# Second MLP up projection: eleven block-product groups on unscaled operands, the norm's row factor multiplied onto outputs

## The chip, the cores and the metric

The kernel runs on one core of a Trainium2 chip. The metric is the device time of one execution in microseconds (us); lower is better. Engine names are those of the profile: PE is TensorE (matmuls), PEld its weight loads, DVE is VectorE, ACT is ScalarE, POOL is GpSimd, SP is SyncE. POOL and SP only issue DMA transfers here. L1068 means line 1068 of the kernel before.

## The reference

One sequence of 512 tokens with 1024 channels goes through two layers: attention and a gated MLP, then a gated short convolution and a gated MLP. Every part has an RMSNorm in front and adds its result to the running state h. The change concerns the second MLP and what stands around it:

```python
def rms_norm(x, g):
    y = xf * lax.rsqrt(jnp.mean(xf * xf, axis=-1, keepdims=True) + EPS)
    return (y * g.astype(jnp.float32)).astype(x.dtype)

def conv_ffn(h, norm_g, w_up, conv_w, w_down):     # D_MODEL 1024, D_FF 2816
    xn = rms_norm(h, norm_g)
    u = causal_dwconv(xn @ w_up, conv_w)            # three taps along the tokens
    g, val = u[..., :D_FF], u[..., D_FF:]
    return (jax.nn.silu(g) * val) @ w_down
```

The norm is a gain for each channel times one factor for each token, 1/sqrt(mean square + EPS). That token factor (the "row factor") commutes with the product by w_up, so it can be multiplied onto xn before the product or onto the outputs behind it. The gain cannot.

## The kernel before, in words

**Numbers.** All data is float32. PE works on operands that are split into two halves, hi (rounded) and lo (the rest), and each product is three matmuls: hi by hi, hi by lo, lo by hi. A weight tile of 128x1024 is split by one ACT copy (whi, L1016) and one DVE subtraction (wlo, L1018). Three buffers of each half turn over.

**The stages.** Layer 0 is attention with its out projection, then MLP 0. Layer 1 is the short convolution (`conv_seven`) with its out projection, then MLP 1. Activations lie transposed, channels on the 128 partitions and the 512 tokens along the free axis.

**Up projection.** The 2816 + 2816 output channels are cut into HF = 11 groups. A group is two 128-channel tiles of the gate and two of the value. Two kinds of groups exist:

- A *plain* group (PLAIN = 2 in each MLP, ahead of the others) is four products of 1024 channels by 512 tokens, 24 matmuls of 512 columns each, with operand halves hs_a, hs_b of h times gain (L360, L361). The row factor is not needed yet; it is multiplied onto the output (`normed`, L1286). While PE works on them, the norm is finished: sums over channels by PE (L398), the reciprocal root by small DVE operations (`scale` L374, L410 to L422), and the spreading of the factor over all partitions (L384, L385).
- A *seven* group (`Sevens`, `seven` L1068) takes one 2x2 block scheme with seven half-size products, called p1, p7, p3, p6, p2, q5, q4. Each is 24 matmuls of 256 columns. Their operands are sums and differences of quarters of the normed activations (channels halved, tokens halved into LEFT and RIGHT), made once by `prepare` from h, gain and row factor (L1270, L1277), in hi and lo. Their weights are sums of blocks of w_up: X, Y, Z, three, W, four.

**The slots of a seven group** (`Sevens.slot`): slot 0 is p1 into bank A, 1 is p7 into T, 2 is p3 of the *previous* group into R, 3 is p6 into R, 4 is p2 into A, 5 is q5 into R, 6 is q4 into T. Around them stand the loads by SP (X, Y, three, W, Z), the splits of the next weights, the copies out of the banks by ACT (`to_wide` L1112 for the LEFT half of the gate yg and value yv; `kept` L1120), the joins by DVE for the RIGHT half (`join` L1115), the three-tap convolutions (`causal_conv`, first tap ACT L431, others DVE L434) and the products of gate and value (L1055, L1056).

**Weight sums.** Some are read from tables in DRAM that POOL's DMAs build ahead (`table_steps`, L102, L105; FAR = 8 steps behind attention, 16 at slot 20 of the convolution). X becomes X plus a block by a POOL DMA that adds while it writes (`add_block`, L1095). "four" is "three" plus W: in MLP 0 it is loaded from a third table, in MLP 1 it is one DVE addition in place (L1179). "three" is read by p6 before that and as "four" by q4 after it.

**The down projection** follows (L1614); its operands are made from the gated outputs, with adding POOL DMAs (L1060).

**What sets the order.** Each engine runs its own instructions in order and waits on semaphores. The order is fixed when the kernel is built, by a scheduler with a cost model; instructions marked with `keep_in_program_order` stay in the order in which the code wrote them. Tiles of a pool with a tag reuse the buffers of that tag, and wait for their last readers.

Of the kernel before, what the change touches and what calls it, by code (L numbers as in the profile page):

```python
# [25 lines left out]
P = 128  # L26
# [23 lines left out]
PLAIN = 2  # L50
FAR = 8, 16
CHUNKS = (2, 3), (5, 3), (8, 3)
# [4 lines left out]
def trunk(  # L57
# [7 lines left out]
    act, dve, pe, pool = nc.scalar, nc.vector, nc.tensor, nc.gpsimd  # L65
# [21 lines left out]
    def table_steps(layer):  # L87

        w = ffn_w_up[layer]
        for n in "76" if layer else "764":  # L90
            for g, m in CHUNKS:
                tables[layer, n, g] = far.tile([512, m * 256 + 16], F32, tag=f"t{layer}{n}{g}", name=f"t{layer}{n}{g}")
        def block(kh, half, g, m):
            return w[kh * 512:(kh + 1) * 512, half * DFF + g * 256:half * DFF + (g + m) * 256]
        for g, m in CHUNKS:
# [12 lines left out]
    def table_of(layer, n, group):  # L108
        g, m = next(c for c in CHUNKS if c[0] <= group < c[0] + c[1])
        return tables[layer, n, g][:, (group - g) * 256:(group - g + 1) * 256].rearrange("(k p) c -> p k c", p=P)  # L110
# [150 lines left out]
    brought, pin = {}, tc.keep_in_program_order  # L261
# [82 lines left out]
    class Norm:  # L344
# [27 lines left out]
        def scale(self, sums):  # L372
# [4 lines left out]
            if self.name != "n0":  # L377
                after(NROWS, self.spread)
# [17 lines left out]
        def finish(self, at=NSUMS):  # L396
            def sums(b, t):
                pe.matmul(t[:, b:b + 1], self.acc[:, b * P:(b + 1) * P], ones, start=True, stop=True)  # L398
                if b == NB - 1:
                    self.scale(t[:, 0:NB])  # L400
# [79 lines left out]
    def want_conv_out():  # L480
        for o in range(ND):
            want(conv_w_out[0], 0, 8, o * P, P)
        want_ffn(1, 2 * PLAIN)

    want_ffn(0, 2 * PLAIN)
# [501 lines left out]
    sum_far(FAR[0])  # L987
# [41 lines left out]
    class Blocks:  # L1029
# [3 lines left out]
        def __init__(self, mp, layer):  # L1033
            self.layer = layer
            self.parts = {0: mp.tile([P, HEAD, S], F32, tag="head", name=f"head{layer}")}

        def at(self, j, n):
            start = 0 if j < HEAD else HEAD if j < HF else HF
            if start not in self.parts:
                shape, tag = ([P, HF - HEAD, S], "hs_b") if start == HEAD else ([P, HF, S], "hs_a")  # L1040
                self.parts[start] = hsp.tile(shape, F32, tag=tag, name=f"{tag}_blocks{self.layer}")
# [20 lines left out]
    def seven(acc, w, x, fresh, last=True):  # L1062
# [8 lines left out]
        spend(2.8)  # L1071

    class Sevens:

        def __init__(self, name, mp, groups, block_of):
            self.name, self.mp, self.groups, self.block_of = name, mp, groups, block_of
            self.forms = {n: [mp.tile([P, 4, HT], F32R, tag=f"{n}_{i}", name=f"{n}_{i}{name}") for i in ("hi", "lo")] for n in FORMS}
            self.st, self.wides, self.table, self.fours = {}, {}, None, False
# [31 lines left out]

        def to_wide(self, g, n, side, acc):
            act.activation(self.wides[g][n][:, :, side], acc.rearrange("p (i t) -> p i t", t=HT), AF.Copy)  # L1112

        def join(self, g, n, acc, other):
            dve.tensor_tensor(  # L1115
                self.wides[g][n][:, :, RIGHT], acc.rearrange("p (i t) -> p i t", t=HT), other.rearrange("p (i t) -> p i t", t=HT), op=ALU.subtract)
# [22 lines left out]
        def slot(self, g, s):  # L1139
# [21 lines left out]
            elif s == 1:  # L1161
                first = not was
                if on and first and not self.ahead:
# [7 lines left out]
            elif s == 2:  # L1171
                if on:
                    self.kept(g, "P7s", c["T"])
                    self.weights_of(g, "p2", "W")
                    if self.fours:
                        self.load_one(g, "four", self.table("4", g))
                    else:
                        c["four"] = c["three" if self.table else "Y"]
                        dve.tensor_tensor(c["four"], c["four"], c["W"], op=ALU.add)  # L1179
# [42 lines left out]
    def up_seven(layer, norm, mp):  # L1222

        blocks = Blocks(mp, layer)
        w_up, base = ffn_w_up[layer], PLAIN
# [8 lines left out]
        up.fours = layer == 0  # L1234
        up.rate = lambda g, s: 1.4 if g == base else 0.3 if layer else 0.5

        def wides_of(g):
# [3 lines left out]
            return {n: mp.tile([P, 2, S], F32, tag=n, name=f"{n}{layer}{g}", bufs=1) for n in ("yg", "yv", "ug", "uv")}  # L1241
        up.wides_of = wides_of
        wides, forms, chores = up.wides, up.forms, up.chores
# [18 lines left out]
        up.tail = tail  # L1262
# [54 lines left out]
    def conv_seven(norm, mp):  # L1317
# [9 lines left out]
        def quarter(n, i, dt, name):  # L1327
            return mp.tile([P, 4, S], dt, tag=f"y_{n}{i}", name=name)
        early_t, early_b = (quarter(n, 0, F32, f"early_{n}") for n in ("hi", "lo"))
# [17 lines left out]
        def open_ys():  # L1347
            ys.append([quarter(n, len(ys), F32R, f"y_{n}{len(ys)}") for n in ("hi", "lo")])
# [47 lines left out]
        def prepare():  # L1396
            x0, x1 = (quarter(n, 1, F32, f"x_{n}") for n in ("hi", "lo"))
# [47 lines left out]
        for s in range(28):  # L1445
            up.slot(1 + s // 7, s % 7)
            if s == 20:
                sum_far(FAR[1])
# [6 lines left out]
        return ys  # L1455

    def mlp(layer, norm, mp):
        blocks, slots = up_seven(layer, norm, mp)
# [62 lines left out]
        n_up = 7 * (HF - PLAIN)  # L1521
        for i, fn in enumerate(slots[:n_up]):
            fn()
            left = n_up - i
# [177 lines left out]
```

## Time and profile before

| what | value |
|---|---|
| time, 3 runs | median 1123.12 us (1122.23 to 1123.92) |
| span of the profiled execution | 1119.7 us |
| median of the runs less that span | 3.4 us |
| granted TensorE clock | 90% of full speed or more in all 40 slices |
| end of the conv out projection in the trace | 779.1 us |
| MLP 1, two plain groups | 779.1 to 825.3 us |
| MLP 1, nine seven groups | 825.3 to 1001.8 us |
| down projection of MLP 1 and the end | 1001.8 to 1119.7 us |

The profiled execution has no time of its own listed beside its span; the 3.4 us between span and median are what lies around it. Start times in rows are microseconds from the start of the span. A row's duration is how long one instruction was in the engine, and because engines pipeline, neighbours may start before it is over: the cadence, start to start, is what counts for a sum. In brackets behind a row stands how long the engine was idle before it, and for whom.

### The profile page before, as it was taken

Reading aid. Unit: us, or ns where it says so; the run is one execution under the profiler, and the core shown is the slowest. Engines: PE = TensorE matmul, PEld = TensorE weight load, DVE = VectorE, ACT = ScalarE, POOL = GpSimd, SP = SyncE. Lnnn points to the kernel's source line nnn. Section 1 sums busy time; section 2 is a strip of 40 time slices with the busy share of each in tenths; the row PEclk is TensorE's granted clock in tenths of the full one; section 3 lists DMA queues with packets and bytes.
Section 4 is the critical chain, followed back from the end, with each engine's and each line's share of the span. In section 5 each row is a group of like instructions: output and inputs, shape, how many; then the busy total and the mean of one; then the engine's idle time right before and its main releaser. Section 6 shows DMA issues by size and latency. Waiting matters only on the chain.

```text
span 1119.7 us, 19368 instructions
## 1 busy us (share of the span) xinstructions
PE 1112.4 (99%) x7659; PEld 1008.0 (90%) x7659; DVE 947.8 (85%) x1463; ACT 680.0 (61%) x1013; POOL 158.4 (14%) x191
## 2 busy tenths in 40 slices
PE   9999999999999999999999999999999999999998
PEld 7888787878899999999999899988899999998876
DVE  6798988987899887888989889865899888898886
ACT  7456676655567667676547355543456766667553
POOL 4111111111111110014400001111101110014300
PEclk9999999999999999999999999999999999999999
DMA  6668878778888687699953456699877666699961
GB/s 195 171 178 193 187 185 198 167 193 207 235 207 200 184 217 192 190 304 194 225 164 91 124 142 140 147 239 227 215 185 186 168 183 152 188 266 194 233 154 57
DMA packets 175690, 209.34 MB, mean 187 GB/s; under 512 B 7564, under 2 KB 140220, under 8 KB 175600
## 3 DMA queue, kind: packets, MB, share of 16 engines
q0 software_dynamic: 41024, 86.95, 39.3%
q1 hardware_dynamic: 134416, 121.09, 34.9%
q8 instruction: 60, 0.98, 0.4%
q14 instruction: 30, 0.25, 0.1%
q10 hardware_dynamic: 160, 0.07, 0.0%
HBM read 203.10 MB, written 49.28 MB: 225 GB/s over the span
## 4 chain that ended last, share of the span: by engine, by line
PE 96%; DVE 2%; ACT 1%; issue 0%; DMA 0%; SPq 0%; DVEq 0%; ACTq 0%
PE psb L1068 28%; PE psa L1068 11%; PE psb L1614 11%; PE psa L1614 8%; PE psb L324 6%; PE psb L326 6%; PE psb L325 6%; PE psa L326 2%; PE psa L324 2%; PE psa L325 2%; PE psb L699 2%; PE psa L796 2%; PE psc L771 1%; PE psc L326 1%; PE psc L325 1%; PE psc L324 1%
## 5 line engine op out<-in xcount | busy, mean ns | idle before, releaser
L303 ACT ACTIVATE whi<-raw 128x1024 fp32r<-128x1024 f32 (+2 forms) x89 | 91.7, 1031 | 97.0 <-PE psb L325 36.6
L304 DVE TENSOR_TENSOR wlo<-raw,whi 128x1024 fp32r<-128x1024 f32 (+2 forms) x89 | 105.5, 1186 | 24.1 <-ACT whi L303 23.4
L1068 PE MATMUL psb<-p_lo,whi_p 128*128 128x256 f32 x432 | 121.6, 282 | 0.0
L1068 PE MATMUL psb<-p_hi,wlo_p 128*128 128x256 f32 x432 | 121.6, 281 | 0.0
L1068 PE MATMUL psb<-p_hi,whi_p 128*128 128x256 f32 x432 | 121.3, 281 | 0.0
L324 PE MATMUL psb<-hs_a,whi 128*128 128x512 f32 x224 | 92.2, 412 | 0.0
L326 PE MATMUL psb<-hs_a,wlo 128*128 128x512 f32 x224 | 88.9, 398 | 0.0
L1068 PEld LDWEIGHTS psb<-p_hi,whi_p 128*128 128x128 f32 x432 | 81.9, 190 | 0.0
L1068 PEld LDWEIGHTS psb<-p_lo,whi_p 128*128 128x128 f32 x432 | 81.3, 188 | 0.0
L1068 PEld LDWEIGHTS psb<-p_hi,wlo_p 128*128 128x128 f32 x432 | 81.2, 188 | 0.0
L1068 PE MATMUL psa<-p_hi,wlo_p 128*128 128x256 f32 x288 | 81.2, 282 | 0.0
L1068 PE MATMUL psb<-q_lo,whi_q 128*128 128x256 f32 x288 | 81.1, 281 | 0.0
L1068 PE MATMUL psa<-p_lo,whi_p 128*128 128x256 f32 x288 | 81.0, 281 | 0.0
L1068 PE MATMUL psb<-q_hi,wlo_q 128*128 128x256 f32 x288 | 81.0, 281 | 0.0
L1068 PE MATMUL psa<-p_hi,whi_p 128*128 128x256 f32 x288 | 80.8, 281 | 0.0
L1068 PE MATMUL psb<-q_hi,whi_q 128*128 128x256 f32 x288 | 80.8, 281 | 0.0
L1614 PE MATMUL psb<-act,whi 128*128 128x256 f32 x352 | 63.1, 282 | 0.1
L434 DVE SCALAR_TENSOR_TENSOR uv<-yv,taps,uv 128x511 f32<-128x511 f32 (+1 forms) x80 | 56.5, 744 | 0.0
L1614 PE MATMUL psb<-whi,act 128*128 128x512 f32 x176 | 56.3, 398 | 0.0
L434 DVE SCALAR_TENSOR_TENSOR ug<-yg,taps,ug 128x511 f32<-128x511 f32 (+1 forms) x80 | 55.5, 744 | 0.0
L1614 PEld LDWEIGHTS psb<-act,whi 128*128 128x128 f32 x352 | 54.2, 189 | 0.5 <-DVE act L1018 0.3
L1068 PEld LDWEIGHTS psa<-p_hi,whi_p 128*128 128x128 f32 x288 | 54.5, 189 | 0.1
(477 smaller groups left out, 3622.7 us busy)
## 6 DMA issues: line engine op xcount, KB each, us to landing
t<-in_ffn_w_up POOLq DMA_DIRECT2D x42, 768.0 KB, 8.0
t<-t POOLq DMA_DIRECT2D x18, 768.0 KB, 4.9
raw<-in_attn_w_in SPq DMA_DIRECT2D x24, 512.0 KB, 5.0
X<-in_ffn_w_up SPq DMA_DIRECT2D x18, 512.0 KB, 5.1
Y<-t SPq DMA_DIRECT2D x18, 512.0 KB, 6.1
three<-t SPq DMA_DIRECT2D x18, 512.0 KB, 3.7
W<-in_ffn_w_up SPq DMA_DIRECT2D x18, 512.0 KB, 4.1
X<-in_ffn_w_up POOLq DMA_DIRECT2D x18, 512.0 KB, 7.7
```

Of the source, the lines that this page charges most:

```text
L303: return (act.activation(hi[:, at_], raw[:, at_], AF.Copy), dve.tensor_tensor(lo[:, at_], raw[:, at_], f32(hi[:, at_]), op=ALU.subtract))
L304: dve.tensor_tensor(lo[:, at_], raw[:, at_], f32(hi[:, at_]), op=ALU.subtract))
L324: made = [pe.matmul(acc, w[0], rhs[0], start=first, stop=False), pe.matmul(acc, w[0], rhs[1], start=False, stop=False), pe.matmul(acc, w[1 ...
L325: pe.matmul(acc, w[0], rhs[1], start=False, stop=False),
L326: pe.matmul(acc, w[1], rhs[0], start=False, stop=last)]
L434: dve.scalar_tensor_tensor(dst[:, d:], src[:, 0:S - d], tap(j), dst[:, d:], op0=ALU.mult, op1=ALU.add)
L699: pe.matmul(ss[e][:, c:c + wide], ql[rows, b * P:n], kl[rows, 0:wide], start=first and b == bs[0], stop=last and b == bs[-1])
L771: pe.transpose(t[:, k * P:(k + 1) * P], w[:, e, k * P:(k + 1) * P], ident)
L796: pe.matmul(out_, w, t[:, first:first + step * (NB - k - 1) + 1:step, :], start=k == 0 and i == 0, stop=k == NB - 1 and i == 1)
L1068: pe.matmul(to, w[a][:, k, c], x[b][:, k, :], start=fresh and i + k + t == 0, stop=i == 1 and k == 3 and t == 2, skip_group_check=not fresh)
L1614: pe.matmul(to, l, r, start=begin and o + t == 0, stop=end and t == 2 and o == (0 if layer else 1), skip_group_check=not fresh)
```

## The change

`PLAIN` becomes a pair: two plain groups in MLP 0, none in MLP 1. In MLP 1:

- All 11 groups are seven groups. Their operands are made from h times gain, without the row factor (`RawForms`: `take` is an ACT copy of each finished h tile, `make` the sum or difference and its split). p1 and p7 are made after tile 3 of the conv out projection, p6 after tiles 5 and 7, and p2, q5, q4, p3 in slots 1, 2, 3 and 5 of group 0. From tile 7 to slot 6 ACT and DVE keep the program's order (`strict`, the wrapper `InOrder`).
- The row factor goes onto outputs (`scaled`). In `to_wide` a DVE multiply takes the place of the ACT copy; each `join` gets a second DVE multiply in place. Four DVE operations of 128x512 a group, two ACT copies fewer.
- "four" is no DVE addition any more: a POOL DMA adds the block of W onto "three" in SBUF, as it is done for X.
- The norm's sums start at a later point (`EARLY`, `LATER`), and `seven` gives the schedule of small PE jobs a chance after every group of three matmuls (`spend(0.35)`) in place of once a product.
- The tables of layer 1 cover all 11 groups: 24 steps in place of 16. 8 are issued behind attention in both kernels; of the others one is issued per MLP 0 group, and what is left at slot 20 of the convolution.
- Some tiles move to a shared pool `rp` so that they live across the border of the stages.

Gone with the plain groups are 192 matmuls of 512 columns, 8 weight loads with their splits, 16 operand halves of h, the four multiplies of `normed`, and the `prepare` of MLP 1.

```diff
-PLAIN = 2
-FAR = 8, 16
-CHUNKS = (2, 3), (5, 3), (8, 3)
+PLAIN = 2, 0
+FAR = 8
+CHUNKS = ((2, 3), (5, 3), (8, 3)), ((0, 3), (3, 4), (7, 4))
+EARLY, LATER = 4.0, 4.0
...
     def seven(acc, w, x, fresh, last=True):
...
-        spend(2.8)
+                spend(0.35)
...
         def to_wide(self, g, n, side, acc):
-            act.activation(self.wides[g][n][:, :, side], acc.rearrange("p (i t) -> p i t", t=HT), AF.Copy)
+            to, acc = self.wides[g][n][:, :, side], acc.rearrange("p (i t) -> p i t", t=HT)
+            if self.scaled:
+                dve.tensor_tensor(to, acc, self.row(side), op=ALU.mult)
+            else:
+                act.activation(to, acc, AF.Copy)
 
         def join(self, g, n, acc, other):
...
+            if self.scaled:
+                dve.tensor_tensor(to, to, self.row(RIGHT), op=ALU.mult)
...
                         c["four"] = c["three" if self.table else "Y"]
-                        dve.tensor_tensor(c["four"], c["four"], c["W"], op=ALU.add)
+                        if self.scaled:
+                            self.add_block(g, "four", 1, 0)
+                        else:
+                            dve.tensor_tensor(c["four"], c["four"], c["W"], op=ALU.add)
...
+    class RawForms:
...
+        def take(self, f):
+            act.activation(self.x[f // 4][:, f % 4, :], h[:, f, :], AF.Copy, scale=gain_of(self.up.norm.base, f))
...
             if o:
                 fetch(AHEAD)
-            residual_out(o, acc, norm)
+            residual_out(o, acc)
         for o in range(2, ND):
             w, acc = weights(), bank("ab"[o % 2])
             out_products(w, acc, range(ND))
-            residual_out(o, acc, norm)
-        norm.finish()
...
+            strict[0] = o == ND - 1
+            residual_out(o, acc)
+            if o == 3:
+                raw.make("p1")
+                raw.make("p7")
+                up.load_pair(0)
+            elif o == 5:
+                raw.make("p6", slice(0, 2))
+            elif o == 6:
+                up.weights_of(0, "p1", "X")
+                up.first_sums(0)
+        norm.finish(EARLY, LATER)
```

How the rows move. First DVE in one steady group of MLP 1, from a product of gate and value to the splitting of "three" for p6. wlo_p and wlo_q are the lo halves of weights, yg and yv the gate and value outputs (in one tile y_both after the change), ug and uv their convolved forms, Xs and P7s sums kept in SBUF. Before:

```order
L1056 SCALAR_TENSOR_TENSOR head_8957<-ug_9501,uv_9502 128x2x256
L1018 TENSOR_TENSOR wlo_p_9751<-X_9575,whi_p_9750 128x1024
L1115 TENSOR_TENSOR yv_9746<-psb_9607,P7s_9640 128x2x256
L1018 TENSOR_TENSOR wlo_p_9783<-Y_9576,whi_p_9782 128x1024
L1115 TENSOR_TENSOR yg_9745<-psb_9582,Xs_9707 128x2x256
L1018 TENSOR_TENSOR wlo_p_9815<-Z_9743,whi_p_9814 128x1024
L434 SCALAR_TENSOR_TENSOR ug_9747<-yg_9745,taps,ug_9747 128x511 x2
L434 SCALAR_TENSOR_TENSOR ug_9747<-yg_9745,taps,ug_9747 128x510 x2
L1018 TENSOR_TENSOR wlo_p_9856<-three_9787,whi_p_9855 128x1024
L1179 TENSOR_TENSOR three_9787<-three_9787,W_9819 128x1024
```

The same stretch of DVE in the changed kernel:

```order
L1066 SCALAR_TENSOR_TENSOR head_blocks_9415<-ug_9662,uv_9663 128x2x256
L1127 TENSOR_TENSOR y_both_9905<-psa_9703,nrow_n_9131 128x2x256
L1029 TENSOR_TENSOR wlo_p_9908<-X_9736,whi_p_9907 128x1024
L1133 TENSOR_TENSOR y_both_9905<-psb_9768,P7s_9801 128x2x256
L1029 TENSOR_TENSOR wlo_p_9938<-Y_9737,whi_p_9937 128x1024
L1135 TENSOR_TENSOR y_both_9905<-y_both_9905,nrow_n_9131 128x2x256
L1133 TENSOR_TENSOR y_both_9905<-psb_9743,Xs_9865 128x2x256
L1135 TENSOR_TENSOR y_both_9905<-y_both_9905,nrow_n_9131 128x2x256
L1029 TENSOR_TENSOR wlo_p_9970<-Z_9901,whi_p_9969 128x1024
L446 SCALAR_TENSOR_TENSOR ug_9903<-y_both_9905,taps,ug_9903 128x511 x2
L446 SCALAR_TENSOR_TENSOR ug_9903<-y_both_9905,taps,ug_9903 128x510
L1029 TENSOR_TENSOR wlo_p_10012<-three_9942,whi_p_10011 128x1024
```

Three of the four multiplies with the row factor (nrow) stand between the products and the splitting of "three", one convolution step has moved behind it, and the addition of W onto "three" is gone from DVE.

Second, DVE at the start of MLP 1, from the last tile of the out projection to the splitting of X for q5 of group 0. All rows bear the line of the wrapper `InOrder`. p_lo and q_lo are lo halves of operands, s_up a scratch sum, hs_a_conv holds h times gain, nv is the first of the 13 small steps of the reciprocal root, which end in ncol. After:

```order
L74 TENSOR_TENSOR h<-psb_8944,h 128x512
L74 TENSOR_TENSOR s_up<-s_up,hs_a_conv 128x512
L74 TENSOR_TENSOR p_lo_8669<-s_up,p_hi_8668 128x512
L74 TENSOR_TENSOR nacc_n_8661<-nacc_n_8661,sq_n_8974 128x512
L74 TENSOR_TENSOR wlo_p_9009<-three_8942,whi_p_9008 128x1024
L74 TENSOR_TENSOR wlo_p_9044<-W_9002,whi_p_9043 128x1024
L74 TENSOR_TENSOR p_lo_8671<-hs_a_conv,p_hi_8670 128x1024
L74 TENSOR_TENSOR s_up<-hs_a_conv 128x1024
L74 TENSOR_TENSOR q_lo_8673<-s_up,q_hi_8672 128x1024
L74 TENSOR_SCALAR nv_n_9063<-psc_9025 128x4
```

What ran beside 46 us of plain products before (the root of the norm, the operands) stands here between the splits of the first block products' weights; the split of X for q5 (wlo_q) comes behind the root.

Third, PE at the same place, from the last matmuls of p2 to the first of q5 of group 0. L396 transposes ncol into the row factor, L1596 transposes h for the last residual. After:

```order
L1078 MATMUL psa_8977<-p_hi_8670,whi_p_9043 128x256
L1078 MATMUL psa_8977<-p_lo_8671,whi_p_9043 128x256
L1078 MATMUL psa_8977<-p_hi_8670,wlo_p_9044 128x256
L396 MATMUL psc_9132<-ident,ncol_n_9065 128x128 x4
L1596 MATMUL psc_11881<-ident,h 128x128 x4
L1596 MATMUL psc_11908<-ident,h 128x128 x4
L1078 MATMUL psb_9041<-q_hi_8672,whi_q_9107 128x256
L1078 MATMUL psb_9041<-q_lo_8673,whi_q_9107 128x256
L1078 MATMUL psb_9041<-q_hi_8672,wlo_q_9108 128x256
```

The transposes of ncol stand in PE's order ahead of q5, so that whatever delays ncol delays all products behind it.

147 lines of the change are left out of this document (102 added, 45 removed).

## The prediction

> **What bounds the kernel now.** I read the page's busy times first, then the chain that ended last, then the stretches of MLP 1, then DVE's own rows in one group.
>
> ```profile
> PE 1112.4 (99%) x7659; PEld 1008.0 (90%) x7659; DVE 947.8 (85%) x1463; ACT 680.0 (61%) x1013; POOL 158.4 (14%) x191
> PE 96%; DVE 2%; ACT 1%; issue 0%; DMA 0%; SPq 0%; DVEq 0%; ACTq 0%
> ```
>
> The first line is busy time, the second the share of the chain by engine. PE is busy for 99% of the span, and the chain runs through PE for 96% of it. So matmuls that disappear are worth their full time, and any new wait of PE costs its full time.
>
> ```profile
> 779.07 0.40 PE L324 MATMUL psa<-hs_a,whi 128*128 128x512 f32 x1
> 779.31 0.39 PE L325 MATMUL psa<-hs_a,whi 128*128 128x512 f32 x1
> ...
> 779.20:825.30 46.10, 46.10 (x207) 37.45 (x206) 39.35 (x67) 22.01 (x32) 5.71 (x7) 1.00 0.87 226
> 825.30:845.20 19.90, 19.90 (x170) 19.90 (x170) 19.64 (x27) 13.57 (x19) 2.48 (x2) 1.00 0.76 176
> 925.20:945.10 19.90, 19.90 (x170) 19.90 (x169) 17.34 (x22) 13.26 (x18) 1.29 (x1) 1.00 0.63 164
> ```
>
> The first two rows are matmuls of the first plain product (start, duration). The other three are stretches, with the busy time of PE, PEld, DVE, ACT and POOL, then granted clock, DMA share and GB/s: the plain groups, the first seven group, a steady seven group. In a steady group PE is full and DVE has 17.34 of 19.90 us to do, so only some 2.6 us are free on DVE. The clock is 1.00 throughout.
>
> **PE: what is removed and added.**
>
> ```profile
> 825.29 2.83 PE psa L1068 x24
> ...
> 933.68 2.85 PE psa L1068 x24
> 936.53 5.67 PE psb L1068 x48
> 942.20 2.85 PE psa L1068 x24
> ...
> 1001.84 8.37 PE psa L1614 x36
> ```
>
> These are pieces of the chain: start, length, matmuls. Plain matmuls of 512 columns start 0.233 us apart (779.07 to 779.31 and on; 192 of them, with the few small ones of the norm, fill the 46.1 us). A block product of 24 takes 2.84 us, 0.1183 us a matmul. Two plain groups are 192 x 0.2333 = 44.8 us. Two seven groups are 14 x 24 x 0.1183 = 39.75 us. The sums and transposes of the norm (the other 1.3 us) stay. PE gains **5.0 us**, the only gain in the change.
>
> [...]
>
> **DVE in a steady group.** Here is a group of before from the split of "three" (as "four") for q4 on (start, duration, and in brackets idle time with whom DVE waited for):
>
> ```profile
> 935.57 1.22 DVE L1018 TENSOR_TENSOR wlo_q<-three,whi_q 128x1024 fp32r<-128x1024 f32 x1
> 936.71 0.74 DVE L434 SCALAR_TENSOR_TENSOR uv<-yv,taps,uv 128x510 f32<-128x510 f32 x1
> 937.49 0.69 DVE L1055 TENSOR_TENSOR hs_a_blocks<-ug,uv 128x512 f32<-128x512 f32 x1
> 938.10 0.69 DVE L1056 SCALAR_TENSOR_TENSOR hs_a_blocks<-ug,uv 128x512 f32<-128x512 f32 x1
> 938.70 1.22 DVE L1018 TENSOR_TENSOR wlo_p<-X,whi_p 128x1024 fp32r<-128x1024 f32 x1
> 939.83 0.69 DVE L1115 TENSOR_TENSOR yv<-psb,P7s 128x512 f32<-128x512 f32 x1
> 940.43 1.22 DVE L1018 TENSOR_TENSOR wlo_p<-Y,whi_p 128x1024 fp32r<-128x1024 f32 x1
> 942.24 0.69 DVE L1115 TENSOR_TENSOR yg<-psb,Xs 128x512 f32<-128x512 f32 x1 [0.58 <-PE psb L1068]
> 943.21 1.23 DVE L1018 TENSOR_TENSOR wlo_p<-Z,whi_p 128x1024 fp32r<-128x1024 f32 x1 [0.28 <-ACT whi_p L1016]
> 944.35 2.73 DVE L434 SCALAR_TENSOR_TENSOR ug<-yg,taps,ug 128x511 f32<-128x511 f32 x4
> 947.00 1.22 DVE L1018 TENSOR_TENSOR wlo_p<-three,whi_p 128x1024 fp32r<-128x1024 f32 x1
> 948.25 1.23 DVE L1179 TENSOR_TENSOR three<-three,W 128x1024 f32<-128x1024 f32 x1
> ```
>
> By start to start, a 128x1024 split costs 1.14 us, a 128x512 operation 0.60, a convolution step 0.66. Each group loses the addition at 948.25 (1.14) and gains four multiplies (2.4): 17.34 + 1.26 = 18.6 us of 19.9. By the sum of busy times alone it still fits.
>
> **The loop through the adding DMA.** It is the order that decides. Before, "three" plus W was DVE's next row. Now DVE splits "three" for p6, POOL then adds W's block by DMA, ACT splits the sum, and DVE does the wlo_q split, which stands in DVE's fixed order *ahead* of all the rows that lead to the next group's split of "three". So the period of DVE cannot be shorter than this loop. From wlo_q on, by the rows above and the order of after: 1.14 + the two products 1.21 + X 1.13 + a join 0.60 + Y 1.14 + a second join 0.60 + three multiplies 1.92 (0.60 each and 0.12, an estimate, for one that needs the result right before it) + Z 1.14 + three convolution steps 2.0 + "three" 1.22 = **12.1 us**.
>
> ```profile
> L1095 POOL DMA_DIRECT2D X<-in_ffn_w_up x8: 1283/1303/1381, 840.2 to 980.0; - x8
> DMA to landing us min/median/max: 6.5/8.1/9.0
> ...
> 940.53 1.29 POOL L1095 DMA_DIRECT2D X<-in_ffn_w_up  x1 [18.85 <-DVE yv L1115]
> ...
> X<-in_ffn_w_up POOLq DMA_DIRECT2D x1, 512.0 KB, 6.9
> 934.21 1.05 ACT L1016 ACTIVATE whi_q<-three 128x1024 fp32r<-128x1024 f32 x1
> ```
>
> The nearest row for the new transfer is X's: the same 512 KB, the same adding form, the same queue, eight times in MLP 1, landing 6.5 to 9.0 us after issue. The issue of 940.53 came 0.0 to 0.6 us after the DVE rows that it may have waited for; I take 0.3. That transfer, with no other POOL transfer before it, landed after 6.9 us. "Three" is added some 8 us behind X, so it too goes mostly alone: I take **7.0**, with 6.5 and 9.0 for the range. ACT's split and two hand-overs are 1.1. The loop is 12.1 + 0.3 + 7.0 + 1.1 = **20.5 us** against PE's 19.9, so PE waits 0.62 us a group. Before, the q4 split was done at 936.79 and q4 began at 936.53 + 2.84 = 939.37, a lead of 2.6 us; the 1.26 us of added DVE work leaves 1.3 of it. Over nine periods (group 0's order is its own): 9 x 0.62 - 1.3 = **+4.3 us** (at 6.5 nearly nothing; at 8.5, 2.1 a period, +17.6).
>
> [...]
>
> **The start of MLP 1.**
>
> ```profile
> 779.27 0.69 DVE L990 TENSOR_TENSOR h<-psb,h 128x512 f32<-128x512 f32 x1 [2.23 <-PE psb L326]
> ...
> 787.09 0.15 DVE L374 TENSOR_SCALAR nv_n<-psc 128x4 f32<-128x4 f32 x1
> ...
> 789.33 0.16 DVE L422 SCALAR_TENSOR_TENSOR ncol_n<-rb_n,ry_n 128x4 f32<-128x4 f32 x1
> ...
> L1112 ACT ACTIVATE yv<-psb 128x512 f32<-128x512 f32 x18 | 10.7, 596 | 16.9 <-PE psb L1068 16.9
> ```
>
> Before, DVE had 46 us of plain products to finish the norm (nv to ncol is 2.4 us). Now, from the last h at 779.27 to the split of Y for p7 of group 1, DVE's order has nine 128x512 rows (5.4), twelve 128x1024 rows (13.7) and the root (2.4): 21.5 us, so 800.8 at the earliest. To that come waits for ACT at places where the next row needs what ACT makes of DVE's last result: h times gain 0.60, the half split of p6 0.60 (both priced like the 596 ns copy above), the splits for q5 and p3 1.05 each, and 1.3, an estimate, for hand-overs and ACT's own queue, in all 4.6: 805.4. Without any wait, PE would start that p7 at 779.1 + 7 x 2.84 + 0.84 (sums) + 1.3 (transposes) = 801.1. PE waits **4.2 us** in all, part of it at the transposes of ncol, which stand ahead of q5 and hold q5, q4 and the next p1 behind them. Bounds: 0, if ACT is ahead everywhere, and 4.6.
>
> **The rest.** At the end, one multiply (0.60) more stands between the last bank and the first operand of the down projection: +0.6, bounds 0 and 1.8 (three).
>
> ```profile
> 760.00:780.00 20.00, 20.00 (x88) 16.15 (x86) 10.55 (x14) 7.56 (x10) 2.33 (x3) 1.00 0.97 236
> 360.00:380.00 20.00, 20.00 (x172) 20.00 (x171) 16.28 (x22) 13.36 (x19) 3.06 (x3) 1.00 0.85 209
> t<-in_ffn_w_up POOLq DMA_DIRECT2D x42, 768.0 KB, 8.0
> ```
>
> The operands of p1, p7 and p6 are made beside the out projection, where DVE has 10.55 busy of 20 us: nothing; uncovered, p6's second half costs the 1.2 us already in the 4.6. Nine table steps move into MLP 0, one a group, into POOL's queue behind X's addition, at a DMA share of 0.85 with DVE at 16.28 of 20 us: nothing; at worst each pushes X by what its 8.0 us exceed X's 7.7, 9 x 0.3 = 2.7. The convolution has seven steps left in place of 16, a relief that PE, full there, does not show.
>
> **The sum**: -5.0 + 4.2 + 0.6 + 4.3 = +4.1 on 1119.7, a span of 1123.8. The median before is 3.4 above the span of its profiled execution; with the same 3.4: **1127 us**.
>
> **Rivals.**
> - *The loop closes in time.* If the addition lands within 19.9 - 13.5 = 6.4 us, DVE keeps up and only the start costs: -5.0 + 4.2 + 0.6 = -0.2, 1122.9 us. For it: landings of 6.5 exist, with other loads beside them. Against: the median of 8.1.
> - *The start is hidden too.* ACT works ahead, the scheduler's pinned order fits: -5.0 + 0.6 = -4.4, 1118.7 us. For it: ACT has 13.3 of 19.9 us to do. Against: 21.5 us of DVE rows in 22.0 us of PE leave 0.5 for all hand-overs. This is the case on the other side, faster; it decides when landing is under 6.4 and the waits for ACT are under 0.5 us.
> - *Additions land as behind other POOL transfers.* W's block now comes from memory twice a group (SP's load and the addition), and at 8.5 us the loop is 22.0: -5.0 + 4.2 + 0.6 + 17.6 = +17.4, 1140.5 us. For it: the median of 8.1. Against: the share of 0.63 leaves room.
> - That the plain groups stay is excluded: no row of theirs is left in the order of after.
>
> **How the numbers follow.** The forecast (landing 6.6 to 7.7: 1123.5 to 1133.5) has a chance of 0.45, the closed loop 0.20, the hidden start 0.20, the long landing 0.15. The range, 1118 to 1134, takes in all but the last. 0.2% is 2.25 us, about what a measurement of this kernel can tell from no change. Faster by that (below 1120.9): the hidden start and a little of the closed loop, 0.23. Within (to 1125.4): the rest of the closed loop and the lower edge of the forecast, 0.25. Slower: 0.52.
>
> **What would show it.** PE should lie in products of 2.84 us from 779 on, with gaps of about 2 us ahead of q5 of group 0 and of p7 of group 1. In the steady groups the wlo_q split of "three" should show idle time that ends with the DMA or with ACT's whi_q, some 2 us each, and the group's period on PE should be 20.5 us in place of 19.9 from group 2 or 3 on. If the period is 19.9 to the end, the loop term is wrong; if PE has no gaps in group 0, the start term is. If products take longer than 2.84 us, or MLP 0 moves, the cause is none of mine.

## The result, and the profile after

The changed kernel takes 1134.85 us (median of 4 runs, 1134.63 to 1135.97) against 1123.08 us: slower by a ratio of 1.0106, 95% interval 1.0092 to 1.0121. The forecast was slower, 1127 us with a range of 1118 to 1134; the time lies 0.85 us above it, and most of it comes from places that the forecast had priced at nothing or next to nothing.

First the page's busy times and the chain's shares by engine, after:

```profile
PE 1115.0 (98%) x7803; PEld 1016.2 (90%) x7803; DVE 957.7 (85%) x1471; ACT 679.8 (60%) x999; POOL 175.9 (16%) x204
PE 90%; DVE 4%; DMA 3%; ACT 1%; issue 1%; SPq 0%; DVEq 0%; ACTq 0%
```

PE's share of the chain falls from 96% to 90%, and DMA, which had 0%, has 3%. PE is busy 2.6 us more, although it has fewer columns to work off: in part because some of its matmuls ran at half the clock (below). The next rows are the DMA pieces of that chain (start, length):

```profile
359.55 13.06 DMA four<-t
...
492.21 10.04 DMA X_chain<-in_ffn_w_down
...
995.40 12.34 DMA three<-in_ffn_w_up
```

Two of the three lie in MLP 0, which the change hardly touches. And this is what PE waited for, by engine and line (total, times, longest), over the whole span; rows under 0.8 us and those of other stages are left out:

```profile
PE psb L1078 <- ACT whi_q L1027: 2.7, 2, 2.5
PE psb L1078 <- DVE wlo_q L1029: 1.9, 3, 0.8
PE psc L396 <- DVE ncol_n L74: 1.5, 1, 1.5
PE psb L1078 <- DVE wlo_p L74: 1.5, 1, 1.5
PE psa L1675 <- DVE wlo L316: 1.5, 2, 0.8
PE psa L1675 <- ACT whi L315: 1.2, 1, 1.2
```

The stages, by the start of the first matmul of each in the PE rows of both traces:

| stage begins | before | after | later by | stage longer by |
|---|---|---|---|---|
| MLP 0, first block product | 319.55 | 319.99 | 0.44 | 3.00 |
| MLP 0, down projection | 495.71 | 499.15 | 3.44 | 3.67 |
| convolution | 608.51 | 615.62 | 7.11 | 0.55 |
| conv out projection | 734.38 | 742.04 | 7.66 | -0.04 |
| MLP 1, up projection | 779.07 | 786.69 | 7.62 | 5.76 |
| MLP 1, down projection | 1001.67 | 1015.05 | 13.38 | -0.16 |
| last matmul ends | 1115.72 | 1128.94 | 13.22 | |

The profile of before was a quick execution: its span is 3.4 us under the median, that of the change 1.95 (1134.85 - 1132.9). So the spans differ by 13.2 us and the medians by 11.8. More than half of the loss stands before MLP 1 begins. Inside MLP 1, PE gained and lost more than it gained. Here are four stretches of it, with the columns of the prediction's windows (the clock is third from the end):

```profile
786.70:808.50 21.80, 20.00 (x165) 19.29 (x164) 16.93 (x28) 12.36 (x16) 2.99 (x3) 1.00 0.52 105
808.50:830.20 21.70, 20.18 (x170) 19.96 (x169) 20.53 (x26) 13.58 (x17) 3.09 (x3) 1.00 0.77 189
830.20:850.10 19.90, 19.90 (x171) 19.90 (x170) 18.69 (x24) 12.27 (x15) 4.09 (x4) 1.00 0.80 191
949.50:969.40 19.90, 19.90 (x171) 19.90 (x170) 18.61 (x24) 12.46 (x15) 2.57 (x2) 1.00 0.75 187
```

The first two groups have holes in PE; the steady ones are full at 19.9 us with DVE at 18.6, to the digit what the sum of DVE's rows had given. So the loop through the addition onto "three" does **not** make PE wait in the steady groups. The single landings show why: a steady one, and the one of the last group, which was issued among the first loads of the down projection.

```profile
three<-in_ffn_w_up POOLq DMA_DIRECT2D x1, 512.0 KB, 5.7
three<-in_ffn_w_up POOLq DMA_DIRECT2D x1, 512.0 KB, 12.3
```

What the last one did (the chain at the end of the up projection, then stretches there):

```profile
995.40 12.34 DMA three<-in_ffn_w_up
...
1007.83 1.06 ACT whi_q L1027
...
1008.91 1.24 DVE wlo_q L1029
...
1010.20 4.85 PE psb L1078 x21
```

```profile
1006.40:1008.90 2.50, 0.04 (x1) 0.00 (x0) 0.00 (x0) 1.07 (x2) 0.00 (x0) 1.00 1.12 269
1010.20:1012.00 1.80, 1.80 (x8) 1.80 (x9) 1.80 (x4) 1.80 (x4) 0.00 (x0) 0.50 1.11 206
1014.00:1015.00 1.00, 1.00 (x6) 1.00 (x6) 1.00 (x2) 0.00 (x0) 0.00 (x0) 0.50 1.01 389
1016.00:1017.00 1.00, 1.00 (x6) 0.83 (x5) 1.00 (x3) 0.13 (x1) 0.00 (x0) 0.99 0.80 248
```

PE waits 2.49 us for the split of "three" by ACT and 0.66 for that by DVE, and its granted clock is 0.50 for 6.8 us, from 1009.18 to 1016.01. q5 and q4 of this group take 1015.05 - 1003.45 = 11.6 us in place of 5.7: a wait of 3.15 us cost 5.9.

### The profile page after: what moved, and what is told of

It is laid out like the page before. It is cut to its first block, busy times and chain, and to the rows that moved or that the text cites. A ratio compares the mean times of both kernels' runs of the same rounds, so it can differ in the third digit from the quotient of the medians.

```text
span 1132.9 us, 19709 instructions
## 1 busy us (share of the span) xinstructions
PE 1115.0 (98%) x7803; PEld 1016.2 (90%) x7803; DVE 957.7 (85%) x1471; ACT 679.8 (60%) x999; POOL 175.9 (16%) x204
## 4 chain that ended last, share of the span: by engine, by line
PE 90%; DVE 4%; DMA 3%; ACT 1%; issue 1%; SPq 0%; DVEq 0%; ACTq 0%
PE psb L1078 28%; PE psb L1675 11%; PE psa L1078 10%; PE psa L1675 8%; PE psb L336 6%; PE psb L338 5%; PE psb L337 5%; PE psb L710 2%; PE psa L338 2%; PE psa L337 2%; PE psa L336 2%; PE psa L807 2%; DMA four<-t 1%; DMA three<-in_ffn_w_up 1%; PE psc L782 1%; DMA X_chain<-in_ffn_w_down 1%
## 5 line engine op out<-in xcount | busy, mean ns | idle before, releaser
L1078 PE MATMUL psb<-p_hi,wlo_p 128*128 128x256 f32 x480 | 135.0, 282 | 1.5 <-DVE wlo_p L74 1.5
L1078 PE MATMUL psb<-p_hi,whi_p 128*128 128x256 f32 x480 | 135.1, 282 | 0.0
L1078 PE MATMUL psb<-p_lo,whi_p 128*128 128x256 f32 x480 | 135.1, 282 | 0.0
L1078 PE MATMUL psb<-q_hi,wlo_q 128*128 128x256 f32 x320 | 91.5, 286 | 1.9 <-DVE wlo_q L1029 1.9
L336 PE MATMUL psb<-hs_a,whi 128*128 128x512 f32 x192 | 79.4, 413 | 0.0
L338 PE MATMUL psb<-hs_a,wlo 128*128 128x512 f32 x192 | 76.2, 398 | 0.0
L1078 PEld LDWEIGHTS psb<-q_hi,whi_q 128*128 128x128 f32 x320 | 61.6, 193 | 3.2 <-ACT whi_q L1027 3.1
L1078 PEld LDWEIGHTS psb<-q_hi,wlo_q 128*128 128x128 f32 x320 | 61.2, 191 | 2.6 <-DVE wlo_q L1029 2.6
L1078 PEld LDWEIGHTS psb<-q_lo,whi_q 128*128 128x128 f32 x320 | 61.3, 191 | 0.0
L1078 PEld LDWEIGHTS psa<-p_hi,wlo_p 128*128 128x128 f32 x320 | 60.1, 188 | 0.2 <-DVE wlo_p L1029 0.2
```

Source lines behind the costliest of these rows:

```text
L336: made = [pe.matmul(acc, w[0], rhs[0], start=first, stop=False), pe.matmul(acc, w[0], rhs[1], start=False, stop=False), pe.matmul(acc, w[1 ...
L338: pe.matmul(acc, w[1], rhs[0], start=False, stop=last)]
L1078: pe.matmul(to, w[a][:, k, c], x[b][:, k, :], start=fresh and i + k + t == 0, stop=i == 1 and k == 3 and t == 2, skip_group_check=not fresh)
```

## The experiments

All are edits of the kernel before or of the changed kernel; the diffs are cut to what differs. "MLP 0", "MLP 1" and so on are the stage lengths of the table above, each against before, by the profiled execution of each kernel. The letters e, f, g and h (with c1) stand for rounds of runs. The kernel before, run again in each round, had medians from 1122.58 to 1123.29 us, so a difference between runs of two rounds is uncertain by some 0.7 us; the ratios go by the kernel before of the same round.

**1. The table steps alone (e1), and elsewhere (e2).** e1 puts the change's timing of the table steps into the kernel before, and nothing else:

```diff
         for i, fn in enumerate(slots[:n_up]):
             fn()
+            if layer == 0 and i % 7 == 6:
+                sum_far(1)
...
-                sum_far(FAR[1])
+                sum_far(99)
```

> The kernel before, with only the issue of the layer 1 table steps moved as in the change: 8 behind attention, one behind each MLP 0 group, the rest at slot 20 of the convolution (same chunks and bytes as before). Theory A (the table steps in MLP 0 delay loads that PE waits for): about +6 us against before, 1127 to 1131 us, with MLP 0 ending 5 to 7 us later and MLP 1 as before. Rival (the late MLP 0 comes from something else in the change, and the steps are hidden): 1123 us, within 1 us of before.

Measured: 1125.56 us, ratio 1.0024 (1.0014 to 1.0033); by spans, MLP 0's up projection +0.64 us, its down projection +3.06, convolution +0.69, MLP 1 +0.01. By the medians it is 2.3 us in all; the spans overstate it, as they do for the change. The steps in MLP 0 do cost, less than expected here, where each carries 768 KB (1024 KB for most in the change). Most of it is at the start of the down projection. The DMA issues there, before and e1 (queue, count, KB, us to landing):

```profile
X_chain<-in_ffn_w_down SPq DMA_DIRECT2D x1, 512.0 KB, 4.1
```

```profile
t<-in_ffn_w_up POOLq DMA_DIRECT2D x2, 768.0 KB, 11.9
...
X_chain<-in_ffn_w_down SPq DMA_DIRECT2D x1, 512.0 KB, 10.9
```

Two table steps behind the last two groups move with the first loads of the down projection, and these land after 9 to 14 us in place of 4 to 10.

e2 takes all nine out of MLP 0:

```diff
+            if j < 6:
+                sum_far(1)       # products at the start of the convolution
...
+            if s in (3, 6, 10, 13, 17):
+                sum_far(1)       # slots of the convolution
```

> The changed kernel, with the nine table steps taken out of MLP 0: six are issued beside the plain products at the start of the convolution, where the DMA share is 0.37, five among its slots, the rest at slot 20. Theory A: MLP 0 is as before, 1127 to 1128.5 us (7 less than the change). Rival 1 (the steps cost the same wherever they stand): 1133 to 1136 us. Rival 2 (the first X addition of MLP 1 comes late behind the steps): PE waits ahead of q5 of group 0, over 1130 us.

Measured: 1139.52 us, ratio 1.0146 (1.0131 to 1.0161), worse than the change. MLP 0's up projection is as before (+0.00), its down projection +1.56, but the convolution is 6.58 us longer: the additions for the convolution's own weights share POOL's queue with the steps and land late (two after 16 to 17 us, where the change has 10 to 11), and PE waits there at q5 (2.30 us) and three other products. An underused DMA share was no free place here.

**2. The last addition (e3), all additions (e4).**

```diff
-                        if self.scaled:
+                        if self.scaled and g < HF - 1:      # e3; e4: if False
                             self.add_block(g, "four", 1, 0)
```

> The changed kernel, with W added onto three by DVE in the last group only, by POOL in the other ten. Theory B (the addition of the last group lands late among the first loads of the down projection, and PE's wait also halves its clock): q5 and q4 of the last group take 5.7 us in place of 11.6, 1128.5 to 1130 us. Rival (the down projection's first loads are late as well, so PE waits a little later for them): 1132.5 to 1135 us.

Measured: 1129.65 us, ratio 1.0059 (1.0044 to 1.0074), 5.2 us less than the change. MLP 1 is 1.23 us longer than before in place of 5.76. PE's waits in it and the down projection:

```profile
PE psb L1078 <- DVE wlo_p L74: 1.5, 1, 1.5
PE psc L396 <- DVE ncol_n L74: 1.5, 1, 1.5
PE psb L1078 <- DVE wlo_q L1029: 0.8, 1, 0.8
PE psc L1596 <- ACT nrow_n L74: 0.3, 1, 0.3
```

The wait for ACT's split at the last q4 is gone, and no wait in the down projection of MLP 1 takes its place. (At the start of MLP 0's down projection, where the change waits 1.19 and 0.76 us, the profiled execution of e3 waits 2.58 and 0.76 and then has 3.4 us of half clock, though the edit does not touch that stage.)

> The changed kernel, with W added onto three by DVE in all eleven groups, as before the change. Theory B (only the last group's addition costs; DVE has 18.6 + 1.1 = 19.7 of 19.9 us to do): 1128.5 to 1131 us, as with the last group alone. Rival (DVE is full, its waits for ACT no longer fit, and the period grows by 0.3 to 1 us a group): 1132 to 1140 us.

Measured: 1131.5 us, ratio 1.0073 (1.0058 to 1.0088), 1.85 us more than e3 (the intervals overlap). Its steady groups show no wait, so DVE, 1.1 us a group fuller, still keeps up there; but the wait at ncol is 2.67 us in place of 1.5, since group 0's addition is one more DVE row in the crowded start. g4 repeats this on the best base (g2, below):

> The kernel of g2, with W added onto three by DVE in all eleven groups. Theory L (the loop with POOL is closed in the steady groups, so nothing is to be gained there; DVE has 1.1 us more to do a group): the same as g2 or up to 1.5 us more. Rival (the second read of W's block and POOL's additions disturb other loads): 1 to 3 us less than g2.

Measured: 1124.38 us, ratio 1.0010 (1.0002 to 1.0019), 1.55 us more than g2 (the intervals overlap), again at the start, where the waits are 1.75, 0.71 and 0.55 us in place of three of 0.6, and 3.4 us of half clock follow the first. So, by the traces, an addition by POOL is worth a DVE row in group 0 (2.67 less 1.52 and 1.75 less 0.61 us, 1.1 both times). In the nine groups after it, it is worth nothing: e3 and g2 each have a wait of 0.76 us there behind a late landing, e4 and g4 none. In the last it costs 5.2 us.

**3. Table steps spread (f1), none in MLP 0 (f2), behind the addition (g1).** f1 is e3 with the two last steps of MLP 0 moved into MLP 1:

```diff
-            if layer == 0 and i % 7 == 6:
+            if layer == 0 and i % 7 == 6 and i < 49:
...
-                sum_far(99)
+                sum_far(7)
...
+            if g in (1, 2) and s == 6:      # slots of MLP 1
+                sum_far(1)
```

> The kernel of e3 (last addition by DVE), with two of the nine table steps of MLP 0, those behind its last two groups, moved into MLP 1 behind its groups 1 and 2. Theory A2 (the steps hurt where they meet the first loads of the down projection, more than in the up projection): the start of MLP 0's down projection loses nothing, 1124 to 1126.5 us. Rival (what counts is the number of bytes that pass in MLP 0): 1128 to 1130 us.

Measured: 1129.35 us, ratio 1.0051 (1.0031 to 1.0072), no better than e3, for another reason than the rival's: MLP 0 recovers (up +0.65, down +0.38), and MLP 1 gives it back (+6.37). POOL's rows there, and PE's longest wait:

```profile
843.90 1.30 POOL L1105 DMA_DIRECT2D X<-in_ffn_w_up  x1 [0.55 <-DVE wlo_p L1029]
844.66 1.49 POOL L114 DMA_DIRECT2D t<-in_ffn_w_up  x1
851.81 1.34 POOL L1105 DMA_DIRECT2D three<-in_ffn_w_up  x1 [5.66 <-DVE wlo_p L1029]
```

```profile
t<-in_ffn_w_up POOLq DMA_DIRECT2D x1, 1024.0 KB, 14.8
...
three<-in_ffn_w_up POOLq DMA_DIRECT2D x1, 512.0 KB, 12.1
```

```profile
PE psb L1078 <- ACT whi_q L1027: 3.2, 1, 3.2
```

With this step ahead of it, the addition onto "three" of group 3 lands after 12.1 us, and the loop of the prediction binds: PE waits 3.22 us at that group's q4. The other step, ahead of the addition of group 2, did no harm: that addition landed after 6.4 us, and PE did not wait.

> The kernel of e3 with no table step in MLP 0: 10 behind attention, 8 at slot 20 of the convolution, 6 in MLP 1, one behind each of its groups 0 to 5. Theory A2: MLP 0 takes as long as before the change, 1122 to 1125 us. Rival (the steps in MLP 1 lengthen the additions onto three beyond 6.4 us and the loop binds): MLP 1 loses 3 us or more, 1126 to 1132 us.

Measured: 1150.19 us, ratio 1.024 (1.0206 to 1.0275). Six groups of MLP 1 have a step ahead of the addition and five of them a wait at q4: MLP 1 +21.6. MLP 0's up projection is 7.31 longer as well, since with ten steps behind attention the X addition of its first block-product group stands behind them, and PE waits 5.26 us ahead of that group's q5. g1 moves f1's two steps behind the addition onto "three" of the same groups (`s == 2` in place of `s == 6`):

> The kernel of f1, with the two table steps of MLP 1 issued right behind the addition onto three of groups 1 and 2, in place of ahead of it. Theory L (the loop through the addition onto three binds when its landing is over 6.4 us; a table step ahead of it lengthens it, one behind it does not): PE's wait at q4 of group 1 and the half clock behind it go, 5 us less than f1, 1123.5 to 1125.5 us. Rival (a table step delays whatever else loads in the group): another wait takes its place, 1127 to 1130 us.

Measured: 1124.74 us, ratio 1.0017 (1.0008 to 1.0025), 4.6 us less than f1; the wait at 861 us is gone (the expectation calls its group 1; by the products ahead of it, it is group 3), MLP 1 is 1.64 us longer than before. So the loop is real: landings of 5.7 us cost nothing, 12.1 us costs 3.2 and a slow clock. Two landings of 7.4 and 7.5 us in a row (groups 3 and 4 of g1), together 2.1 us over the 6.4 of the prediction, cost PE 0.6 us; the prediction's lead of 1.3 us would account for the rest.

**4. Only the tables (g3).** The changed kernel with the steps placed as in g1:

> The changed kernel with only the table steps placed as in g1; the addition onto three stays with POOL in the last group too. If the three losses of the change (tables in MLP 0, the start of MLP 1, the last addition) are independent, it is 5 to 6.5 us faster than the change: 1128.5 to 1130 us, and its MLP 1 takes as long as that of the change. Rival (the losses cover one another): less than 3 us faster, over 1132 us.

Measured: 1133.3 us, ratio 1.009 (1.0074 to 1.0106): only 1.5 us less than the change (the intervals overlap). By spans MLP 1 begins 4.0 us earlier than in the change, but its last wait grows from 2.49 to 4.42 us, and MLP 1 from +5.76 to +7.93. The losses are not independent: behind e3's edit the same move of the steps is worth 4.9 us (1129.65 to 1124.74). Why the last addition is later relative to PE can be read from the chain of g3, two additions of which are these (issue, landing):

```profile
974.28 5.97 DMA three<-in_ffn_w_up
...
993.80 12.78 DMA three<-in_ffn_w_up
```

The second is issued 13.55 us behind the landing of the first. From group 2 on, all intervals between issues in g3 are a landing plus 13.5 to 13.7 us, in the change a landing plus 13.5 to 14.1. So DVE goes at the pace of this loop even where PE does not wait, and a landing over 6.4 us makes the next additions late. g3 has three of them (7.7, 7.0 and 6.9 us in groups 3, 4 and 7), the change one (6.8 us), and from group 2 to the last group the additions of g3 take 160.1 us, those of the change 157.7. Why those three landed late stays open.

**5. The start of MLP 1 (f3, g2, f4, h1).** f3 is f1, g2 is g1, with the norm's root behind the splits for q5:

```diff
-EARLY, LATER = 4.0, 4.0
+EARLY, LATER = 8.0, 4.0
...
-                    self.left(g, c["A"])
+                    if not (self.scaled and g == 0):
+                        self.left(g, c["A"])      # group 0: one slot later
```

> The kernel of f1, with the norm's sums and root put behind the splits for q5 of group 0 on DVE, and the transposes of ncol behind q5 on PE; the first row-factor multiply moves one slot back for it. Theory C (the sum of DVE's work up to the split of Y of group 1 sets the start, 4.6 us behind PE): the wait ahead of q5 goes, and that at p7 of group 1 grows by as much, within 0.8 us of f1. Rival (the order does it: ncol's transposes hold PE for nothing): 1.5 to 2 us less than f1.

Measured: 1129.91 us, ratio 1.0056 (1.0038 to 1.0074), level with f1; but its wait behind group 3's addition is 4.96 us in place of 3.22 in the profiled runs, which hides the start. At the start the waits of f1 (1.52 and 1.52) became three of 0.6.

> The kernel of g1, with the norm's root put behind the splits for q5, as in f3. By f3's trace (waits of 1.85 us at the start in place of 3.04): 1.2 us less than g1, 1122.3 to 1124.5 us, level with the kernel before. Rival (theory C, DVE's sum sets the start): within 0.5 us of g1.

Measured: 1122.83 us, ratio 1.0000 (0.9991 to 1.0010), 1.9 us less than g1. The order was worth 1.4 us of the start's 3.3 us of waits in the traces. f4 moves the two subtractions for q5 and p3 from DVE to POOL:

> The kernel of f3, with the two subtractions that make the operands of q5 and p3 on POOL in place of DVE. Theory C: DVE has 2.3 us less to do before the split of Y of group 1, and PE waits 1.5 to 2.3 us less than in f3. Rival (ACT's splits wait longer for POOL's slower subtraction, or DVE slows beside POOL): the same as f3 or more.

Measured: 1130.47 us, ratio 1.0062 (1.0042 to 1.0083), no less than f3. Both waits at ncol and at p7 are gone, and a new one of 3.04 us stands in p6, and 6.8 us of half clock begin in it. DVE's and POOL's rows:

```profile
787.21 2.11 DVE L74 TENSOR_TENSOR p_lo<-s_up,p_hi 128x512 fp32r<-128x512 f32 x1 [0.70 <-ACT p_hi L74]
789.85 3.37 DVE L74 TENSOR_TENSOR wlo_p<-three,whi_p 128x1024 fp32r<-128x1024 f32 x1
793.14 1.21 DVE L74 TENSOR_TENSOR wlo_p<-W,whi_p 128x1024 fp32r<-128x1024 f32 x1
```

```profile
785.87 2.90 POOL L1314 TENSOR_TENSOR s_up<-hs_a_conv 128x1024 f32<-128x1024 f32 x1 [1.30 <-ACT hs_a_conv L74]
789.41 2.73 POOL L1314 TENSOR_TENSOR s_up<-hs_a_conv,s_up 128x1024 f32<-128x1024 f32 x1 [0.63 <-DVE p_lo L74]
```

The two DVE operations that meet POOL's take 2.11 and 3.37 us in place of 0.7 and 1.2. h1 is g2 with the same sum eased in another way, half of p2's and q4's operands made beside the out projection:

```diff
                 raw.make("p6", slice(0, 2))
+                raw.make("p2", slice(0, 2))
+                raw.make("q4", slice(0, 2))
```

> The kernel of g2, with the first halves of the operands of p2 and q4 made beside tile 5 of the out projection, where DVE is busy for half the time. Theory C2 (what is left of the start's waits, 1.85 us in g2's trace, is the sum of DVE's work): 1 to 1.5 us of the waits go, 1121 to 1122.3 us. Rival (what is left are hand-overs between ACT and DVE): within 0.4 us of g2, 1122.4 to 1123.2 us.

Measured: 1121.38 us, ratio 0.9989 (0.9981 to 0.9998): the start's waits are 0.64 and 0.42, MLP 1 is 2.34 us shorter than before, and the kernel is the fastest of this study, by 0.1%.

**6. Fewer steps in MLP 0 (h2), and the clock by itself (c1).** h2 is h1 with three steps in MLP 0 and six in MLP 1, behind the additions:

> The kernel of h1, with three table steps in MLP 0 in place of seven and six in MLP 1, one right behind the addition onto three of each of its groups 0 to 5. Theory A3 (a step behind that addition is free, one in MLP 0 costs 0.2 us): 0.5 to 1.2 us less than h1, 1120 to 1121.5 us, under the kernel before. Rival (a step a group lengthens the additions of X or three beyond the loop): MLP 1 has new waits at q5 or q4, over 1123 us.

Measured: 1124.63 us, ratio 1.0016 (1.0006 to 1.0025). MLP 0 is as before (within 0.02 us), but MLP 1 has waits again at q4 of group 7 (0.97 and 0.76 us at 939 us) although the steps stand behind the addition, and the clock halves behind them (columns as above):

```profile
939.30:942.80 3.50, 1.77 (x13) 1.49 (x13) 2.47 (x4) 2.90 (x3) 0.00 (x0) 1.00 0.03 5
942.90:946.20 3.30, 3.30 (x18) 3.30 (x17) 3.30 (x5) 0.70 (x1) 1.28 (x1) 0.50 0.95 305
946.40:949.00 2.60, 2.60 (x24) 2.60 (x23) 2.57 (x4) 0.97 (x3) 0.00 (x0) 1.00 1.17 276
```

The additions of groups 6 and 7 landed after 7.7 and 8.2 us, over the 6.4 of the loop; why, with no step beside either, was not settled. c1 is the kernel before with extra work on DVE:

```diff
                         dve.tensor_tensor(c["four"], c["four"], c["W"], op=ALU.add)
+                        for _ in range({3: 4, 6: 5, 9: 6}.get(g, 0) if self.table else 0):
+                            dve.tensor_tensor(c["four"], c["four"], c["four"], op=ALU.max)
```

> The kernel before, with 4, 5 and 6 added DVE operations of 128x1024 (each leaves its data as it is) on W plus three of groups 3, 6 and 9 of MLP 1, ahead of the split for q4: PE waits there, some 1 to 2 us in group 3, 2 to 3 in group 6, 3 to 4 in group 9. Theory H (the clock halves behind a wait of more than about 3 us and stays low for some 6 us): 1.00 throughout behind group 3's wait, 0.50 behind group 9's. Rival (the clock fell in the change for a reason of its own): 1.00 behind all three, and the time grows by the waits alone.

Measured: 1132.56 us in one run. No wait over 0.25 us in group 3; 0.78, 0.44 and 0.25 us in group 6; 2.58 and 0.43 us in group 9. Stretches behind the second and the third (columns as above):

```profile
924.30:927.00 2.70, 2.03 (x14) 1.82 (x15) 2.70 (x5) 1.32 (x2) 0.88 (x1) 1.00 0.12 17
...
984.90:987.50 2.60, 0.03 (x1) 0.00 (x0) 2.57 (x4) 1.10 (x2) 0.00 (x0) 1.00 0.00 0
...
990.00:993.00 3.00, 3.00 (x16) 3.00 (x15) 2.35 (x3) 0.00 (x0) 1.28 (x1) 0.50 0.64 174
993.00:996.00 3.00, 3.00 (x28) 3.00 (x27) 2.36 (x3) 2.33 (x4) 0.00 (x0) 0.99 1.08 168
```

The clock halves behind a wait, in a kernel that has nothing of the change: the rival falls. Of theory H, the 6 us did not come: 0.50 lasted 3.4 us here, and 16 matmuls went through in 3 us of it where 28 do otherwise.

## Why the prediction was right or wrong

- **PE's gain of 5.0 us: right.** The steady groups keep 19.9 us with two groups more of them, and h1, with 1.05 us of waits left, has MLP 1 2.34 us shorter than before. (Of what is missing to 5.0, about 1 us more are the norm's sums and the transposes, which take 2.2 us in MLP 1 after the change and 1.25 before.)
- **The start, +4.2: right in place, kind and size.** PE waited at the transposes of ncol (1.54 and 0.26) and at p7 of group 1 (1.52), 3.3 us by these rows, which count idle time only from the end of the matmul before. From start to start it is 4.3: groups 0 and 1 take 43.5 us (the first two stretches above), and 13 products of 2.84 us with 2.2 us of sums and transposes would take 39.2. DVE took 26.5 us from the last h (786.89) to the end of Y's split (813.4), where 26.1 were forecast. Of those 26.1, 1.3 us were an estimate for hand-overs with no row behind it, so that it came this close is in part luck. That the sum of DVE's rows sets it was half of the truth: their order was worth 1.3 us by MLP 1's length and 1.9 by the medians (g1 to g2), their sum 2.6 and 1.45 (g2 to h1).
- **The loop, +4.3: wrong.** The step that failed is the landing of 7.0 us, taken from X's additions. In groups 2 to 9 of the change, the additions onto "three" landed after 5.7 to 5.9 us, one after 6.8, nearly all under the 6.4 that the text gave as the point where the loop closes. X's additions, in the same groups, took 6.0 to 9.9. The mechanism stands (f1, f2 and g1 switch it on and off), and the rest of the loop, 13.5 us, is what the traces show (13.5 to 14.1 from landing to next issue); the landing chosen was too high. This was the first rival's condition. (The loop's 0.12 us for a multiply that needs the result right before it stood without a row; in the change such a multiply starts 0.72 us behind its join, 929.87 to 930.59, where other rows of that size start 0.60 apart.)
- **The end, +0.6: wrong, the largest single miss.** It priced one multiply, and asked of the new DMA only what it costs in a steady group. In the last group it is issued among the down projection's first loads, lands after 12.3 us, and the wait drags the clock down: 5.9 us, of which e3 gives back 5.2 by the medians.
- **The table steps, "nothing; at worst 2.7": wrong.** The text compared landings (8.0 against 7.7) and asked only whether X's addition is pushed. What suffered were SP's loads beside the steps: four<-t 13.1 us in place of 7.7, X_chain 10.0 in place of 4.1; MLP 0 and the convolution lost 7.2 us by spans, of which PE's rows name 4.1 as waits. A DMA share of 0.85 was read as room. The prediction's own sign that its account was not complete, "or MLP 0 moves", was there.
- The third rival's time of 1140 us came from long landings of "three" in *all* groups; in groups 2 to 10 only the last was that long.

So the forecast's sign was right by luck: without the loop's 4.3 us its sum is -0.2, no change, and what made the kernel slower were two terms priced at 0.6 and 0 that were worth 5.9 and some 5 to 7 us (2.3 in e1, with its smaller steps).

## What to carry to other kernels

A new transfer in a loop has to be priced in the first and the last turn by what loads there, not by the steady turn (the addition onto "three" landed after 5.7 us in a steady group and after 12.3 in the last). Background transfers that are "hidden" are paid by the landings of the loads beside them (X_chain 10.9 us in e1 in place of 4.1): where the next stage's first loads start, keep them out, and issue them behind what is waited for, not ahead of it: POOL's transfers landed in the order of their issue in the traces of before (all 160) and of the change (all 173). Waits of PE should be priced with the clock that may fall behind them: 3.15 us of them cost 5.9 in the last group of the change, and in h2 3.4 us at half clock followed 0.97 and 0.76 us (next section).

## What the runs showed of the hardware that was not expected

**The clock behind a wait.** In the clock records of the change's trace, the granted clock changes at 5.67, 1009.18, 1016.01 and 1132.06 us from the start of the span: 294, 2 and 34 times 3.413 us apart. In those of before it changes at 4.42 and 1120.58, 327 times 3.413 us apart. A stretch of 0.50 lasts 3.41 us (c1, e2, e3, e4, f1, g4, h2) or 6.83 (the change, f3, f4, g3; f2 has both); three of the long ones had waits in their own first half, 0.66 us in the change, some 0.7 in f4 and 2.6 in g3. If the span is cut into steps of 3.41 us that begin and end where the clock changes, the step just ahead of the half clock held 1.65 us of PE's waits in h2, 1.73 in c1, 1.75 in g4, some 2.1 in g3 and 2.49 in the change. In MLP 1 of these five traces, no other step at full clock held more than 1.55 (the change, from 797.56 us). One stretch of 0.50, at 58 us in e4, has only 0.55 us of waits ahead of it and stays unexplained. So, by these traces, what counts is how the waits lie on the steps. 0.97 and 0.76 us, all but 0.08 of it in one step, halved the clock (h2). 2.67 us (e4), 2.30 (e2), 1.94 + 0.75 (f2) and 1.54 + 0.26 (the change, at 799 to 801 us), each spread over two steps, left it at 1.00. What makes the steps was not shown. The prediction priced waits at their length alone.

**DVE beside POOL.** Two DVE splits went from 0.7 and 1.2 us to 2.11 and 3.37 us while POOL subtracted (f4). The first began at 787.21, beside POOL's first subtraction, which ended at 788.77, and ended at 789.32, 0.55 us behind that. The second began at 789.85, beside POOL's second, which ended at 792.14, and ended at 793.22, 1.08 us behind. Both are near the split's own length, as if it had waited for POOL and then run: an inference from these two pairs of rows. The DVE row of 128x512 that began at 789.25, ahead of POOL's second subtraction (789.41), kept its 0.68 us.
